# Stick-breaking attention on (key, query) blocks, with the reverse running sum as products accumulated in PSUM

## The chip, the cores and the metric

One core of one Trainium2 chip runs the whole program. The metric is the time of one execution on the device, in microseconds (us). TensorE (PE) multiplies matrices and accumulates in PSUM banks; VectorE (DVE) and ScalarE (ACT) work element by element on PSUM and SBUF; GpSimd (POOL) does the same for SBUF; SyncE (SP) issues the DMA transfers. In the traces a line such as L1129 is a line of the kernel.

## The reference

An encoder of two layers for 512 prompt frames and 64 sample frames with 1024 cached positions. Each layer is a half step of SwiGLU, a mixer of four head groups side by side on one projection, and another half step of SwiGLU:

```
x = x + 0.5 * swiglu(rmsnorm(x))
h = rmsnorm(x) @ w_in
x = x + concat[mla(h), dsa(h), stick(h), diff(h)] @ w_out
x = x + 0.5 * swiglu(rmsnorm(x))
```

The change concerns the third group, four heads of 64 dimensions:

```
z = einsum('bqhd,bkhd->bhqk', q, k) * 64 ** -0.5
mask = k_pos < q_pos
log_keep = where(mask, log_sigmoid(-z), 0)
log_after = cumsum(log_keep, axis=3, reverse=True) - log_keep
a = where(mask, exp(log_sigmoid(z) + log_after), 0)
out = einsum('bhqk,bkhd->bqhd', a, v)
```

With softplus(z) = -log_sigmoid(-z) and log_sigmoid(z) = z - softplus(z), the weight of key k is exp(z_k - sum of softplus(z_j) over the keys j >= k that the mask admits). So a running sum over the keys, from the last to the first, stands between the scores and the weights.

## The kernel before

The mixer (mix) has two stages. The first is a list of steps, PLAN: index parts, then the latent attention (mla) beside the projections of the stick group, then stick(), then the projections of the differential group (diffp) beside the top-k search of the sample, then the top-k search of the prompt (tp, lines 798 and 799 on DVE) beside the projections of the sparse group (dsap). The second stage has the product with W_out (line 915) of the first and third group beside the attention of the other two, and then W_out of these. Steps are written one after the other, and merge() interleaves the generators of one step. A scheduler then sets the order on each engine from the program's dependences and buffers, so that instructions of a later step can stand ahead of those of an earlier one. The PSUM pools hand out their banks in the order in which the program asks for them: psA has two banks (scores), psG two (projections and W_out), psT two (transposes), psQ one (transposes of queries and keys), psO one (values).

Projections go through win(): for a token tile, each of eight chunks of the input adds three products (lines 444 to 446, high and low parts of both operands) of 256 columns to one psG bank; the sample tile uses lines 432 to 435. A layer's differential and sparse projections are 1184 such products.

stick() loads keys and values, turns the keys (kT: head and dimension by key), and goes through four query tiles of 128 and two pairs of heads. For one tile and pair, scores of two heads are queries by keys (line 1129), the mask is a product that adds a triangle (line 1131), and the scaled scores are copied to SBUF by ACT (line 100). stick_weights() then works on both heads at once: minimum with 30 (line 1145, DVE), Exp and Ln on ACT (1146, 1147), maximum with z (1148, DVE), for each head a scan that sums backwards along the keys (1151, DVE), the sum with z (1152, DVE), and Exp (1153, ACT). The weights are turned to key by query through psT (line 104, copies at lines 88 and 90) and multiplied with the values (line 553). sample() does the same for a pair of heads of the 64 sample frames over 1088 keys. For a query tile, load_q() brings the queries from DRAM through tag q, which has two buffers, and qT() turns them.

The scale, the copies and the splitting of results into a high and a low part (put_o, lines 559 and 560) are helpers that all groups share.

## Time and profile before

| what | us |
|---|---|
| three runs | 2668.05, 2668.62, 2670.72 (median 2668.62) |
| profiled execution, its span | 2668.6 |
| PE busy | 2567.7 (96%) |
| DVE busy | 1471.6 (55%) |
| ACT busy | 1010.9 (38%) |
| first stick score product, layer 0 and 1 | 639.7, 1956.7 |
| first W_out product, layer 0 and 1 | 735.3, 2052.0 |
| end of the mixer, layer 0 and 1 | 911.6, 2229.1 |

A share of busy time is a mean over stages: most of the span is SwiGLU, where PE alone is full (line 324, 63% of the chain that ended last). The mixer is where other engines come near their limits, so it is read by windows of time. A matrix product with F32 operands appears as two records of the same line, one with F32R operands as one. Busy time of PE contains pipelining: the step from the start of one instruction to the start of the next tells more of its cost than its duration.

### The profile page before, as it was taken

The page shows a single profiled execution, that of the slowest core. Times are in us where ns is not written, and L with a number is a line of the kernel's source. Part 1 is how long each engine was busy: PE and PEld are TensorE (multiplying, and loading weights), DVE is VectorE, ACT ScalarE, POOL GpSimd, SP SyncE. Part 2 cuts the span into 40 slices and gives each one's busy share as a digit, 9 for nine tenths or more (in the row PEclk, how much of TensorE's full clock was granted, in tenths as well). Part 3 has the DMA queues.
Part 4 walks back from the last instruction along what each step waited for, and adds up shares of the span by engine and source line. Part 5 has one row for each costly group of instructions (what it writes and reads, how often), then busy time and mean ns, then how long its engine had stood idle before and what let it go on. Part 6 is the DMA issues. An engine that isn't in the chain of part 4 may idle for free.

```text
span 2668.6 us, 45104 instructions
## 1 busy us (share of the span) xinstructions
PE 2567.7 (96%) x18673; PEld 2407.0 (90%) x18673; DVE 1471.6 (55%) x2684; ACT 1010.9 (38%) x1915; POOL 251.6 (9%) x309
## 2 busy tenths in 40 slices
PE   8999999999898899999999999999998889999998
PEld 7999999887775899999999999988877668999998
DVE  5434344799976743433443343458899676434343
ACT  4212124645666522222332222355456664212122
POOL 0000002201410300000100000022015103000001
PEclk9999999999998999999999999999999999999999
DMA  4232323253240222222222222233342203232322
GB/s 136 80 88 80 87 74 115 61 144 90 66 120 18 85 82 85 83 84 83 84 80 86 81 86 81 88 101 91 94 116 83 82 25 95 80 87 80 88 76 72
DMA packets 424348, 227.90 MB, mean 85 GB/s; under 512 B 93980, under 2 KB 419792, under 8 KB 424144
## 3 DMA queue, kind: packets, MB, share of 16 engines
q1 hardware_dynamic: 424144, 225.02, 29.3%
q8 instruction: 147, 2.41, 0.4%
q14 instruction: 57, 0.47, 0.1%
HBM read 206.25 MB, written 18.73 MB: 84 GB/s over the span
## 4 chain that ended last, share of the span: by engine, by line
PE 83%; DVE 9%; ACT 4%; DMA 1%; issue 1%; POOL 1%; SPq 0%; ACTq 0%; DVEq 0%; POOLq 0%
PE psF L324 63%; PE psG L915 2%; PE psT L104 2%; PE psQ L104 2%; PE psO L553 2%; PE psG L444 2%; PE psG L445 2%; PE psG L446 2%; DVE P L1151 1%; PE psO L610 1%; PE psA L1000 1%; DVE P L1198 1%; ACT whl L306 1%; DVE whl L307 1%; PE psA L724 1%
## 5 line engine op out<-in xcount | busy, mean ns | idle before, releaser
L324 PE MATMUL psF<-aH,whl 128*128 128x288 f32 x5632 | 978.3, 295 | 0.0
L324 PEld LDWEIGHTS psF<-aH,whl 128*128 128x128 f32 x5632 | 825.9, 188 | 0.4 <-ACT whl L306 0.2
L306 ACT CAST whl<-raw 128x1024 fp32r<-128x1024 f32 (+2 forms) x342 | 351.7, 1028 | 1046.1 <-PE psF L324 1001.8
L324 PE MATMUL psF<-aL,whl 128*128 128x288 f32 x2816 | 602.5, 295 | 0.0
L324 PE MATMUL psF<-h,whl 128*128 128x288 f32 x4224 | 561.2, 294 | 0.0
L324 PEld LDWEIGHTS psF<-h,whl 128*128 128x128 f32 x4224 | 559.0, 188 | 0.0
L324 PEld LDWEIGHTS psF<-aL,whl 128*128 128x128 f32 x2816 | 450.2, 188 | 0.1
L307 DVE TENSOR_TENSOR whl<-raw,whl 128x1024 fp32r<-128x1024 f32 (+1 forms) x326 | 391.1, 1200 | 28.1 <-ACT whl L306 7.0
L354 DVE TENSOR_TENSOR u<-psF,R 128x576 f32<-128x576 f32 x88 | 66.7, 757 | 368.4 <-PE psF L324 368.4
L370 DVE SCALAR_TENSOR_TENSOR xT<-psF,xT 128x576 f32<-128x576 f32 x96 | 72.7, 757 | 329.1 <-PE psF L324 329.1
L444 PE MATMUL psG<-whl,aH 128*128 128x256 f32 (+1 forms) x672 | 200.4, 299 | 5.7 <-DVE gq L825 3.6
L446 PE MATMUL psG<-whl,aL 128*128 128x256 f32 (+1 forms) x672 | 202.1, 301 | 0.0
L445 PE MATMUL psG<-whl,aH 128*128 128x256 f32 (+1 forms) x672 | 198.4, 295 | 0.9 <-DVE whl L307 0.9
L269 POOL TENSOR_TENSOR ssum<-ssum,sq 128x576 f32<-128x576 f32 x24 | 36.9, 1538 | 1664.3 <-ACT sq L267 1664.3
L352 DVE TENSOR_TENSOR g<-psF,R 128x576 f32<-128x576 f32 x88 | 66.6, 757 | 206.9 <-PE psF L324 198.7
L915 PE MATMUL psG<-op,whl 128*128 128x288 f32 x768 | 133.2, 312 | 14.2 <-ACT op L1232 8.0
L444 PEld LDWEIGHTS psG<-whl,aH 128*128 128x128 f32 x672 | 127.2, 190 | 13.0 <-issue 6.3
L445 PEld LDWEIGHTS psG<-whl,aH 128*128 128x128 f32 x672 | 127.6, 190 | 6.8 <-issue 2.8
L446 PEld LDWEIGHTS psG<-whl,aL 128*128 128x128 f32 x672 | 127.5, 190 | 5.7 <-issue 4.2
L915 PEld LDWEIGHTS psG<-op,whl 128*128 128x128 f32 x768 | 110.6, 194 | 22.2 <-ACT op L1232 8.5
L357 ACT CAST h<-u 128x576 fp32r<-128x576 f32 x88 | 59.4, 674 | 167.5 <-DVE u L355 167.5
L358 DVE TENSOR_TENSOR h<-u,h 128x576 fp32r<-128x576 f32 x88 | 66.7, 758 | 63.2 <-ACT h L357 63.2
(379 smaller groups left out, 2847.6 us busy)
## 6 DMA issues: line engine op xcount, KB each, us to landing
raw<-in_w_ff_gate SPq DMA_DIRECT2D x88, 512.0 KB, 3.7
raw<-in_w_ff_up SPq DMA_DIRECT2D x88, 512.0 KB, 3.7
raw<-in_w_ff_down SPq DMA_DIRECT2D x64, 512.0 KB, 3.6
raw<-in_w_in SPq DMA_DIRECT2D x36, 512.0 KB, 3.7
raw<-in_w_ff_down SPq DMA_DIRECT2D x32, 384.0 KB, 3.2
raw<-in_w_out SPq DMA_DIRECT2D x48, 256.0 KB, 3.3
xs<-xT SPq DMA_DIRECT2D x16, 288.0 KB, 2.1
xT<-xs SPq DMA_DIRECT2D x8, 576.0 KB, 4.3
```

Source lines behind the costliest of these rows:

```text
L104: self.nc.tensor.transpose(out, in_, self.ident[:rows, :rows])
L306: self.nc.scalar.copy(hi[:, 0:n], raw[:, 0:n])
L307: (eng or self.nc.vector).tensor_tensor(lo[:, 0:n], raw[:, 0:n], hi[:, 0:n], ALU.subtract)
L324: mm = nc.tensor.matmul(ps[:, j, 0:HALF], w[c], a(c)[:, hs[j]], start=(c == 0 and p == 0), stop=(c == n - 1 and p == 2))
L352: nc.vector.tensor_tensor(j2(g), pss[0][:, :, 0:HALF], R2, ALU.mult)
L354: nc.vector.tensor_tensor(j2(u), pss[1][:, :, 0:HALF], R2, ALU.mult)
L358: nc.vector.tensor_tensor(h[:, 1, :], u, h[:, 0, :], ALU.subtract)
L370: nc.vector.scalar_tensor_tensor(j2(xv), ps[:, :, 0:HALF], 0.5, j2(xv), ALU.mult, ALU.add)
L444: nc.tensor.matmul(ps[:m, 0:n], a, hi, start=(c == 0), stop=False)
L445: nc.tensor.matmul(ps[:m, 0:n], a, lo, start=False, stop=False)
L446: nc.tensor.matmul(ps[:m, 0:n], b, hi, start=False, stop=(c == KC - 1))
L915: nc.tensor.matmul(ps[k][:, 0:HALF], wt[:, sl], a[:, hs[k]], start=(c == 0 and p == 0), stop=(c == n - 1 and p == 2))
```

## The change

stick() computes scores with keys on the partitions and queries along the row. All five query tiles are loaded and turned first, with the scale 1/8 on the way, into one buffer qT. prompt() takes a pair of heads at a time and the key blocks 3, 2, 1, 0; block b meets the queries from 128 b on, so it has 512 - 128 b columns. Scores stay in their PSUM bank: blocks 3 and 1 in psA, blocks 2 and 0 in psG. softplus() reads the bank, as Abs, Exp and Ln on ACT and one operation on DVE that adds the maximum of z and 0. Into the same bank go products of a matrix of minus ones (negones, for each later key block) and of a triangle of minus ones (negtri, for the block itself) with the softplus values; one Exp then leaves the weights key by query, as the value product takes them. sample() works alike on 9 key blocks in three banks; the later blocks' softplus values are added up by DVE before one product with negones. The scan, stick_weights(), the turning of weights and the copies of the scores go. Both new matrices and their operands are F32.

```diff
@@ -159,9 +159,11 @@
                                 base=0, channel_multiplier=1)
         self.tri = C("triR", [128, 128], F32R)
         nc.vector.tensor_copy(self.tri, tri)
-        self.triS = C("triS", [128, 64], F32R)
-        nc.vector.tensor_copy(self.triS[0:64], tri[0:64, 0:64])
-        nc.vector.tensor_copy(self.triS[64:128], tri[64:128, 64:128])
+        self.negones = C("negones", [128, 128])
+        nc.vector.memset(self.negones, -1.0)
+        self.negtri = C("negtri", [128, 128])
+        nc.gpsimd.affine_select(self.negtri, self.negones, pattern=[[-1, 128]], compare_op=ALU.is_ge, fill=0.0,
+                                base=0, channel_multiplier=1)
         self.rope64 = C("rope64", [128, 5, 2, 32])
         nc.sync.dma_start(self.rope64, I["rope64"])
         self.rope32 = C("rope32", [128, 5, 2, 16])
...
@@ -1085,75 +1087,98 @@
                 self.transpose(pt[:, pr * 128:pr * 128 + 128], kn[:, tt * 256 + pr * 128:tt * 256 + pr * 128 + 128])
             self.evac(self.turn(tt), kT3[:, :, tt * 128:tt * 128 + 128], pt[:, 0:256].rearrange("p (a n) -> p a n", a=2))
         o += self.new_o()
-        def qT(tt, m):
+        qT = self.op()[:, 0:1024].rearrange("p (a n) -> p a n", a=2)
+        for tt, (t0, m) in enumerate(TT):
             q = self.load_q("c", tt, m)
             pt = self.psQ()
             for pr in range(2):
                 self.transpose(pt[:, pr * 128:pr * 128 + m], q[:m, pr * 128:pr * 128 + 128])
-            return pt[:, 0:256]
+            p3 = pt[:, 0:256].rearrange("p (a n) -> p a n", a=2)
+            if tt < 4:
+                self.scaled(qT[:, :, t0:t0 + 128], p3, 0.125)
+            else:
+                for j in range(2):
+                    hs = slice(64 * j, 64 * j + 64)
+                    self.scaled(self.qbds[hs, :, hs], p3[hs, :, 0:64], 0.125)
+
+        def prompt(pr):
+            X, Y = [self.big() for _ in range(2)], [self.big() for _ in range(2)]
+            Z = [t([128, 512], tag="PT") for _ in range(2)]
+            off = {3: 0, 2: 128, 1: 384}
+            part = lambda T, j, b: T[j][:, off[b]:off[b] + 512 - 128 * b] if b else Z[j]
+            for b in (3, 2, 1, 0):
+                N = 512 - 128 * b
+                for j in range(2):
+                    hs = slice(64 * j, 64 * j + 64)
+                    z = (self.psA() if b % 2 else self.psG())[:, 0:N]
+                    nc.tensor.matmul(z, kT[hs, pr * 512 + 128 * b:pr * 512 + 128 * b + 128], qT[hs, pr, 128 * b:512],
+                                     start=True, stop=False)
+                    nc.tensor.matmul(z[:, 0:128], self.tri, self.identR, start=False, stop=True)
+                    sp = part(X, j, b)
+                    self.softplus(sp, z)
+                    for b2 in range(3, b, -1):
+                        nc.tensor.matmul(z[:, (b2 - b) * 128:N], self.negones, part(X, j, b2), start=False, stop=False,
+                                         skip_group_check=True)
+                    nc.tensor.matmul(z, self.negtri, sp, start=False, stop=True, skip_group_check=True)
+                    nc.scalar.activation(part(Y, j, b), z, AF.Exp)
+            po = self.psO()
+            for b in range(4):
+                for j in range(2):
+                    c0 = b * 256 + (2 * pr + j) * 64
+                    nc.tensor.matmul(po[64 * j:64 * j + 64, 128 * b:512], vn[:, c0:c0 + 64], part(Y, j, b),
+                                     start=(b == 0), stop=(b == 3))
+            self.put_o(o, pr, 0, 512, po)
 
         def sample(pr):
-            kTs, vc = sreg[pr]
             self.kT_sample("sb", pr, ksn, kTs)
             self.load_cache("sb", pr, 1, vc)
-
-            def mms(out, s):
-                new = s.start == PAST
-                nc.tensor.matmul(out, self.qbds[:, pr, :], kTs[:, s], start=True, stop=not new)
-                if new:
-                    nc.tensor.matmul(out, self.identR, self.triS, start=False, stop=True)
-            z, a = self.big(), self.big()
-            for ps, s in self.sample_scores(mms):
-                self.scaled(z[:, s], ps, 0.125)
-            self.stick_weights(z[:, 0:LS], a[:, 0:LS], [a[:, 0:LS]])
-            PT = self.pT_sample(a)
+            S, E = self.big(), self.big()
+            blk = lambda T, b: T[:, b * 128:b * 128 + 128]
+            nc.gpsimd.memset(blk(E, 7)[64:128], 0.0)
+            regs = [(self.psT()[0:64, 0:128], 8, 9), (self.psA(), 4, 8), (self.psA(), 0, 4)]
+            for z, b0, b1 in regs:
+                for b in range(b0, b1):
+                    w = 64 if b == 8 else 128
+                    nc.tensor.matmul(blk(z, b - b0), kTs[:, b * 128:b * 128 + w], self.qbds[:, pr, :],
+                                     start=(b == b0), stop=(b < 8), skip_group_check=True)
+                    if b == 8:
+                        nc.tensor.matmul(z, self.tri[0:64, 0:64], self.dupl[0][0:64, :], start=False, stop=True,
+                                         skip_group_check=True)
+                rows = slice(0, 64) if b0 == 8 else slice(0, 128)
+                sp = S[rows, b0 * 128:b1 * 128]
+                self.softplus(sp, z)
+                if b0 == 8:
+                    nc.vector.tensor_copy(blk(E, 7)[0:64], sp)
+                else:
+                    for b in range(b1 - 2, b0 - 2, -1):
+                        if b >= 0:
+                            nc.vector.tensor_tensor(blk(E, b), blk(E, b + 1), blk(S, b + 1), ALU.add)
+                    nc.tensor.matmul(z, self.negones, E[:, b0 * 128:b1 * 128], start=False, stop=False,
+                                     skip_group_check=True)
+                nc.tensor.matmul(z, self.negtri[rows, rows], sp, start=False, stop=True, skip_group_check=True)
+                nc.scalar.activation(sp, z, AF.Exp)
             po = self.psO()
-            self.av_sample(po[:, 0:128], PT, lambda j: vc[:, j * 128:j * 128 + 128], vsn[:, pr * 128:pr * 128 + 128])
+            self.av_sample(po[:, 0:128], S.rearrange("p (b n) -> p b n", n=128),
+                           lambda j: vc[:, j * 128:j * 128 + 128], vsn[:, pr * 128:pr * 128 + 128])
             for j in range(2):
                 self.put_o(o, pr, 512, 64, po[64 * j:64 * j + 64, 64 * j:64 * j + 64], 64 * j, 64 * j + 64)
 
-        sreg = [(kTs, vc)] * 2
-        p3 = qT(4, 64).rearrange("p (a n) -> p a n", a=2)
-        for j in range(2):
-            nc.scalar.copy(self.qbds[64 * j:64 * j + 64, :, 64 * j:64 * j + 64], p3[64 * j:64 * j + 64, :, 0:64])
-        for tt, (t0, m) in enumerate(TT[:4]):
+        for pr in range(2):
             yield
-            L = t0 + 128
-            q = t([128, 512], tag="qT")[:, 0:256]
-            nc.scalar.copy(q, qT(tt, m))
-            for pr in range(2):
-                z, a = self.pair(), self.pair()
-                zv, av = z[:, :, 0:L], a[:, :, 0:L]
-                for j in range(2):
-                    pa, hs = self.psA(), slice(64 * j, 64 * j + 64)
-                    nc.tensor.matmul(pa[:, 0:L], q[hs, pr * 128:pr * 128 + 128], kT[hs, pr * 512:pr * 512 + L],
-                                     start=True, stop=False)
-                    nc.tensor.matmul(pa[:, L - 128:L], self.identR, self.tri, start=False, stop=True)
-                    self.scaled(z[:, j, 0:L], pa[:, 0:L], 0.125)
-                self.stick_weights(zv, av, [a[:, j, 0:L] for j in range(2)])
-                PT = [self.pT_prompt(a[:, j, :], tt, j) for j in range(2)]
-                po = self.av_prompt(PT, lambda kt, j: vn[:, kt * 256 + (2 * pr + j) * 64:
-                                                         kt * 256 + (2 * pr + j) * 64 + 64], tt)
-                self.put_o(o, pr, t0, 128, po[:, 0:128])
-                yield
-            if tt in STICK_AT:
-                sample(STICK_AT.index(tt))
-
-    def stick_weights(self, z, a, rows):
-        """a = exp(z + reverse inclusive sum of -softplus(z)); softplus(z) = max(z, ln(1 + exp(min(z, 30))))"""
-        nc = self.nc
-        nc.vector.tensor_scalar(a, z, 30.0, None, ALU.min)
-        nc.scalar.activation(a, a, AF.Exp)
-        nc.scalar.activation(a, a, AF.Ln, bias=1.0)
-        nc.vector.tensor_tensor(a, z, a, ALU.max)
-        for r in rows:
-            rev = r[:, ::-1]
-            nc.vector.tensor_tensor_scan(rev, self.zero.to_broadcast(list(r.shape)), rev, 0.0, ALU.add, ALU.subtract)
-        nc.vector.tensor_tensor(a, z, a, ALU.add)
-        nc.scalar.activation(a, a, AF.Exp)
+            prompt(pr)
+            yield
+            sample(pr)
+
+    def softplus(self, out, z):
+
+        nc = self.nc
+        nc.scalar.activation(out, z, AF.Abs)
+        nc.scalar.activation(out, out, AF.Exp, scale=-1.0)
+        nc.scalar.activation(out, out, AF.Ln, bias=1.0)
+        nc.vector.scalar_tensor_tensor(out, z, 0.0, out, ALU.max, ALU.add)
...
-STICK_AT = (0, 1)
...
-    nc = bacc.Bacc("TRN2", target_bir_lowering=False, num_devices=1)
+    nc = bacc.Bacc("TRN2", target_bir_lowering=False, num_devices=1, dynamic_dma_scratch_size=4096)
```

Elsewhere the diff takes out comment lines alone. From line 163 on, lines are two higher in the kernel after: 444 to 446 become 446 to 448. The order of the instructions changes on all engines from the last part of the latent attention to the end of the mixer, and nowhere else.

On PE, before, in the stick group of layer 0: products of the differential projections (psG from whl) stand between a tile's transposes (psT from P), the scores of the next tile (L1129) and the values (L553).

```order
L446 MATMUL psG_7325<-whl_7314,aL_3809 128x256
L444 MATMUL psG_7325<-whl_7314,aH_3808 128x256
L104 MATMUL psT_6618<-ident,P_6601 128x128 x2
L104 MATMUL psT_6623<-ident,P_6601 128x128 x2
L445 MATMUL psG_7325<-whl_7315,aH_3808 128x256
L446 MATMUL psG_7325<-whl_7314,aL_3809 128x256
L444 MATMUL psG_7325<-whl_7320,aH_3808 128x256
L445 MATMUL psG_7325<-whl_7321,aH_3808 128x256
L1129 MATMUL psA_6748<-xT_6416,qT_6739 128x384
L553 MATMUL psO_6628<-PT_6621,xT_6416 64x128
```

Six projection products lie between the transposes and around them; in the whole group there are 254 of them.

On PE, after, in the stick group of layer 0: the scores are L1114, the mask L1116, products with the full matrix L1120 and with the triangle L1122.

```order
L1120 MATMUL psA_6704<-P_6660,negones 128x128
L1120 MATMUL psA_6704<-P_6660,negones 128x256
L1122 MATMUL psA_6704<-P_6660,negtri 128x384
L1116 MATMUL psA_6715<-identR,triR 128x128
L1114 MATMUL psG_6738<-op_6449,xT_6417 128x512
L1120 MATMUL psG_6726<-P_6660,negones 128x128
L1120 MATMUL psG_6726<-P_6660,negones 128x256
L1120 MATMUL psG_6726<-P_6660,negones 128x384
L1122 MATMUL psG_6726<-PT_6664,negtri 128x512
L1120 MATMUL psA_6715<-P_6661,negones 128x128
L1120 MATMUL psA_6715<-P_6661,negones 128x256
L1122 MATMUL psA_6715<-P_6661,negtri 128x384
```

The group's own products follow one another, those of one head pair in banks of psA and psG by turns; no projection is among them.

On PE, after, at the end of that group: the last products of the second pair's block 0, and what follows.

```order
L1120 MATMUL psG_6738<-P_6661,negones 128x128
L1120 MATMUL psG_6738<-P_6661,negones 128x256
L1120 MATMUL psG_6738<-P_6661,negones 128x384
L1122 MATMUL psG_6738<-PT_6665,negtri 128x512
L446 MATMUL psG_6861<-whl_6850,aH_3809 128x256
L447 MATMUL psG_6861<-whl_6851,aH_3809 128x256
L448 MATMUL psG_6861<-whl_6850,aL_3810 128x256
L446 MATMUL psG_6861<-whl_6850,aH_3809 128x256
L447 MATMUL psG_6861<-whl_6851,aH_3809 128x256
L448 MATMUL psG_6861<-whl_6850,aL_3810 128x256
```

The first product of the differential projections (L446, bank psG_6861) stands behind the last triangle product of the bank psG_6738; from here on 448 projection products precede the first of W_out.

## Rows read from the trace of the kernel before

**Rows 1.** The page: span, and busy us of each engine.

```profile
span 2668.6 us, 45104 instructions
PE 2567.7 (96%) x18673; PEld 2407.0 (90%) x18673; DVE 1471.6 (55%) x2684; ACT 1010.9 (38%) x1915; POOL 251.6 (9%) x309
```

**Rows 2.** Lines 1129, 915, both layers: ns min/median/max, first and last start (us).

```profile
L1129 PE MATMUL psA<-xT,qT x32: 272/481/694, 639.7 to 712.8; 64*128 64x128 f32 x8, 64*128 64x256 f32 x8, 64*128 64x384 f32 x8, 64*128 64x512 f32 x8
L915 PE MATMUL psG<-op,whl x192: 289/295/405, 735.3 to 791.9; 128*128 128x288 f32 x192
L1129 PE MATMUL psA<-xT,qT x32: 272/481/693, 1956.7 to 2029.7; 64*128 64x128 f32 x8, 64*128 64x256 f32 x8, 64*128 64x384 f32 x8, 64*128 64x512 f32 x8
L915 PE MATMUL psG<-op,whl x166: 288/296/408, 2052.0 to 2099.9; 128*128 128x288 f32 x166
```

**Rows 3.** Windows: stretch, us, busy PE, PEld, DVE, ACT, POOL, PEclk, DMA share, GB/s.

```profile
580.00:640.00 60.00, 59.98 (x419) 45.98 (x417) 52.70 (x155) 29.64 (x88) 7.11 (x13) 1.00 0.29 75
640.00:736.00 96.00, 88.95 (x626) 73.16 (x625) 93.26 (x165) 58.73 (x123) 38.76 (x44) 0.98 0.31 85
1956.00:2052.00 96.00, 89.26 (x632) 73.46 (x631) 93.76 (x168) 58.73 (x125) 39.74 (x44) 0.98 0.32 86
```

**Rows 4.** Costliest DVE lines of 640:736: busy us, mean ns | idle before.

```profile
L1151 DVE TENSOR_TENSOR_SCAN P<-zero,P 128x128 f32<-128x128 f32 (+4 forms) x18 | 18.3, 1052 | 0.0
L799 DVE MATCH_REPLACE8 S<-m,S 128x512 f32<-128x512 f32 (+1 forms) x23 | 14.6, 634 | 0.0
L798 DVE MAX8 m<-S 128x8 f32<-128x512 f32 (+1 forms) x22 | 14.3, 648 | 0.2
L1152 DVE TENSOR_TENSOR P<-P,P 128x256 f32<-128x256 f32 (+4 forms) x10 | 9.7, 970 | 0.0
L1148 DVE TENSOR_TENSOR P<-P,P 128x256 f32<-128x256 f32 (+4 forms) x10 | 9.5, 953 | 0.0
...
L1145 DVE TENSOR_SCALAR P<-P 128x256 f32<-128x256 f32 (+4 forms) x10 | 7.2, 725 | 0.0
```

**Rows 5.** The chain that ended last, in 597:640, its shares by line.

```profile
by line: PE psA L1000 14.9%; PE psO L553 12.3%; PE psT L104 11.2%; PE psA L1024 9.8%; PE psA L1023 8.4%; PE psG L446 8.3%; PE psG L444 7.9%; PE psG L445 7.1%; PE psO L610 4.2%; PE psQ L104 4.1%; PE psQ L1014 2.7%; PE psG L435 2.2%; PE psG L
```

**Rows 6.** PE's instructions in order, 615.0 to 618.3: start us, us, line.

```profile
615.01 0.28 PE L446 MATMUL psG<-whl,aL 128*128 128x256 f32 x1
615.13 0.28 PE L444 MATMUL psG<-whl,aH 128*128 128x256 f32 x1
615.25 0.28 PE L445 MATMUL psG<-whl,aH 128*128 128x256 f32 x1
615.37 1.02 PE L1023 MATMUL psA<-op,ql 128*128 128x512 f32 x2
616.23 1.04 PE L104 MATMUL psT<-ident,P 128*128 128x128 f32 x8
617.19 1.12 PE L1024 MATMUL psA<-op,qT 32*128 32x512 f32 x2
618.24 1.10 PE L553 MATMUL psO<-PT,xT 128*64 128x128 f32 x16
```

**Rows 7.** Score evictions and PSUM copies of 640:760, by form: busy us, mean ns.

```profile
L100 ACT ACTIVATE P<-psA 128x512 f32<-128x512 f32 x8 | 4.6, 592 | 0.0
...
L100 ACT ACTIVATE P<-psA 128x384 f32<-128x384 f32 x4 | 1.8, 492 | 0.0
...
L90 DVE COPY PT<-psT 128x512 f32<-128x512 f32 x2 | 1.4, 684 | 0.6 <-PE psT L104 0.6
...
L90 DVE COPY PT<-psT 128x384 f32<-128x384 f32 x2 | 1.1, 556 | 0.0
```

**Rows 8.** DMA of 600:660: the query tiles' loads, KB each, us to landing.

```profile
q<-qc SPq DMA_DIRECT2D x3, 128.0 KB, 2.1
```

**Rows 9.** Windows behind the group, columns as in rows 3.

```profile
800.00:860.00 60.00, 48.23 (x274) 33.37 (x274) 39.94 (x119) 36.77 (x105) 0.00 (x0) 0.86 0.09 23
736.00:912.00 176.00, 151.64 (x1002) 121.75 (x1003) 128.14 (x335) 113.97 (x311) 34.63 (x24) 0.94 0.25 72
```

## The prediction

> **What bounds the kernel now.** I read the shares of the engines first, then the stretch in which the changed code runs, then the chain into it, then single instructions. TensorE is busy 96% of the span of 2668.6 us [rows 1], so time is mostly PE work, and a change is worth what it does to PE's stream. The page shows one execution; its span equals the median of the three runs (2668.62) to 0.1 us and nothing lies around it, so sums made against the span hold for the median.
>
> The stick-breaking group stands between its first score product and the first W_out product: 639.7 to 735.3 us in layer 0 and 1956.7 to 2052.0 in layer 1, 95.6 and 95.3 us [rows 2]. The reader should see two full engines there: DVE busy 93.26 of 96 us and PE 88.95, ACT only 58.73 [rows 3]. Of DVE's time 44.7 us are the four operations of the running sum (L1151 18.3, L1152 9.7, L1148 9.5, L1145 7.2) and 28.9 us the top-k search (L798, L799) [rows 4]. PE can be full although its attention products wait for DVE, because projections of the differential and sparse groups (L444 to L446) are laid between them: of 1184 such products per layer, the order has 848 ahead of the first stick product, 254 inside the stick group and 82 behind it. Ahead of it, in 580:640, PE is without a gap (59.98 of 60) and DVE has 52.70 [rows 3]; projections take a quarter of the chain there (8.3+7.9+7.1+2.2%) [rows 5].
>
> **The change, part by part, for one layer.**
>
> 1. *The order of the projections.* prompt() takes both psG banks for its key blocks 2 and 0, and the pool hands banks out in program order. So in the changed order no projection stands inside the stick group; 736 are ahead of it and 448 behind it in one run, all before the first W_out product. They step by 0.12 us (615.01 to 615.13) [rows 6]. Between the first stick product and W_out PE therefore gets 448 in place of 336: 112 x 0.12 = +13.4 us. The same 13.4 us leave the stretch ahead, where they will not all be won: what remains there waits for DVE, whose work there is unchanged. Bounds: nothing, and the projections' share of the chain, 25.5% of 43 us, 11 us [rows 5]; DVE's idle time in 580:640 is 7.3 us [rows 3]. I take -6, next to the last.
>
> 2. *Products.* Gone are 40 prompt and 18 sample transposes: four (eight records) step from 616.23 to 617.19, 0.24 us each [rows 6], -13.9. New are products with minus ones: prompt 24 with the full matrix and 16 with the triangle, 5120 columns each; sample 2048 and 2304 columns; 14592 columns in all. Matrices and operands are F32 like L1023, of which 512 columns show two records and step 0.86 us (615.37 to 616.23) [rows 6]: 1.68 ns a column, +24.5. Sample scores by key block are 18 products of 128 columns at 0.24 us, 4.3 us, in place of 2176 columns, 3.7: +0.6. The prompt's own score and value products keep their columns (one of 512 columns costs 694 ns at most as a record [rows 2]; head pairs still write separate halves). Sum +11.2.
>
> 3. *DVE.* 44.7 us go. 22 softplus operations come, reading PSUM at no more than 0.684 us (a PSUM copy of 512 columns [rows 7]), under 15 us, and 14 additions of 128 columns, some 4 us. So DVE loses at least 26 us. That is worth what PE lost by waiting in the old group, 96-88.95 = 7.05 and 96-89.26 = 6.74 [rows 3]: -6.9, all of which I grant, because the new waits are counted apart.
>
> 4. *New waits.* The scores stay in their bank until softplus is back: Abs, Exp, Ln on ACT, one DVE operation, then the minus-ones products, a last Exp, and the value products. PE works in order and has no projections left to lay between. Half of the cover is the other head and the next key block. Per prompt half: the last 512-column block has three ACT passes of 0.592 us and 0.684 on DVE [rows 7], 2.5 us, with nothing ready behind it but the sample's scores; the last Exp before the value product 0.6; the 384-column block has 3x0.49+0.56 = 2.0 [rows 7], less the two products ahead of it (384 and 512 columns at 1.68 ns), 1.5: 0.5. That is 3.6, twice 7.2. The five query tiles are now loaded together through two buffers, 2.1 us to landing [rows 8], ahead of all scores; before, each stood beside the previous tile's work: +1.8. The following projections, dense as they are, wait 1.5 for weights and the first bank. Sum 10.5. Bounds: half the hand-offs hidden, 4; and 22, worked out under the second rival. The nearest row is the old window itself, with DVE still searching top-k between softplus operations, so I stay near the counted value.
>
> 5. *Elsewhere.* Over 736:912 PE is idle 176-151.64 = 24.4 us [rows 9], some of it behind DVE. A DVE that arrives with less behind it may give some back: bounds 0 and 5, taken 1. ACT loses the scaled evictions and gains three passes a block, at most 0.592 us each [rows 7]; with 58.73 us busy in 96 before [rows 3] it stays off the bound in sum, so I count nothing beyond item 4. Set-up of the two constants is a few operations, nothing.
>
> Sum per layer: 13.4+11.2-6.9+10.5-6-1 = +21.2; both layers +42.4; 2668.6+42.4 = 2711.
>
> The Trainium skill ("Perfetto Trace Analysis", Identifying the Most-Contended Engine) says to find the engine with the highest occupancy in a regime and to optimise that one first. In the old window that is DVE with 93.26 of 96 us [rows 3], which speaks for this change: by that rule 26 us less on DVE would shorten the stretch. The trace bears it only to the 7 us that PE waits there. The same page (Optimization Strategy) says that regimes with different limits may gain from being interleaved; the old order interleaves projections with DVE's scans and the new one parts them, and by that rule the change loses.
>
> **The rivals.**
>
> *Faster: the relief of DVE decides.* Place: the stretch ahead, and the two of 736:912. If the attention there falls to PE's own rate, the whole 13.4 us comes back in item 1, new waits shrink to 3, and half of the 24.4 us idle behind [rows 9] goes: 13.4+11.2-6.9+3-13.4-12 = -4.7, twice, 2659. It decides from the point where the stretches outside the group give back over 21 us a layer. For it: DVE 93.26 of 96, 52.70 of 60 [rows 3]. Against it: PE is at 59.98 of 60 ahead of the group, and in 800:860 DVE has only 39.94 of 60 [rows 9].
>
> *Slower still: PE starves in the stick group.* Its own work there is about 49 us: the 88.95 less 336 projections of 0.12 leave 48.6; item 2 makes it 59.8; some 11 of these (the last value products, part of the sample's minus ones, mask products of the sparse group) stand in the changed order behind the first of the 448 projections. Where the old kernel runs attention with hand-offs and few projections, 800:860, PE is busy 48.23 of 60 us and the granted clock is 0.86 of full speed (a mean of its levels 1.2 and 2.4 GHz), PE having waited a fifth of the time [rows 9]. At 0.80 x 0.86 the 49 us take 71, 22 us of waits in place of 9: +34.2 with the 1.5, items 1 and 5 kept, 2668.6+2x34.2 = 2737. For it: the same bank-to-bank pattern. Against it: here two heads and two pools alternate, and 512-column products of 0.86 us are long beside the gaps.
>
> The Trainium skill ("TensorE: Matmul & The Clock Gate", A second HAM failure mode: psum-queue depth-cycling) says that short idles between groups of products, as a kernel cycles through banks, make the clock swing between its two levels. The row of 800:860 agrees with its 0.86; by that rule this rival holds, and by the old window's 0.98 it does not.
>
> *No change.* The added products cost half, as single-pass ones (12.2 in place of 24.5), and the stretch ahead gives back 10 in place of 6: 21.2-12.3-4 = +4.9, with new waits of 6 instead of 10.5 +0.4: 2669. Against it: every F32 product in the trace shows two records.
>
> That the change does not do what it says is not a rival: the scans are gone from the order and the matrices are F32 in the code.
>
> **How the numbers follow.** What this kernel's measurement can tell from no change is 0.2%, 5.3 us. Chances: forecast 0.66, starving 0.21, relief of DVE 0.08, no change 0.05; so faster 0.08, same 0.05, slower 0.87. Range: low end with waits of 4, 11 back ahead and 5 behind, 13.4+11.2-6.9+4-11-5 = +5.7, 2680, which I lift to 2684 since these three would have to fall together; high end with waits of 22 and nothing back ahead or behind, 13.4+11.2-6.9+22 = 39.7, 2748.
>
> **What would show it.** Right: no projections between the stick products, 448 of them in some 53 us behind; the stretch from the first stick product to W_out 124 us instead of 95.6; DVE about 55% busy there; the first stick product about 6 us earlier; minus-ones products of two records, 0.86 us for 512 columns. Wrong: the stick part without projections under 50 us (then the waits are covered), a granted clock under 0.9 in it (the starving rival), the first stick product over 10 us earlier or the stretch behind W_out more than 5 us shorter (relief), or one record per product.

## The result and the profile after

The changed kernel takes 2752.67 us (median of 4 runs, 2743.60 to 2754.99), the kernel before in the same comparison 2669.67. The ratio is 1.0305, with a 95% interval of 1.0291 to 1.0318. That is 83 us slower, where 42 were forecast, and 4.7 us beyond the upper end of the range. The profiled execution has a span of 2749.5 us, 80.9 over that of before.

The page, first lines: PE's busy time is up by 62 us against [rows 1], DVE's down by 52.

```profile
span 2749.5 us, 45258 instructions
PE 2629.6 (96%) x18709; PEld 2432.0 (88%) x18709; DVE 1419.9 (52%) x2632; ACT 1013.7 (37%) x1950; POOL 235.9 (9%) x314
```

The stick group's scores and the W_out products, layer 0 and layer 1, as in [rows 2]:

```profile
L1114 PE MATMUL psA<-op,xT x16: 272/482/587, 638.5 to 697.1; 64*128 64x128 f32 x8, 64*128 64x384 f32 x8
L917 PE MATMUL psG<-op,whl x160: 290/296/401, 773.7 to 819.2; 128*128 128x288 f32 x160
L1114 PE MATMUL psA<-op,xT x16: 272/482/587, 1999.3 to 2051.2; 64*128 64x128 f32 x8, 64*128 64x384 f32 x8
L917 PE MATMUL psG<-op,whl x94: 288/295/402, 2127.9 to 2149.9; 128*128 128x288 f32 x94
```

From the first score to W_out there are now 135.2 and 128.6 us in place of 95.6 and 95.3. Counted from the mixer's first projection, the first score comes 1.9 us earlier in layer 0 and 0.1 in layer 1. From the first W_out product to the end of the mixer there are 4.4 and 4.5 us more. These three make 42.1 and 37.7, all but 1 us of the difference.

Windows of layer 0, columns as in [rows 3]: ahead of the group, the group, the projections behind it, and 174 of the 181 us from W_out to the end of the mixer.

```profile
580.00:638.50 58.50, 49.97 (x314) 32.16 (x312) 53.39 (x157) 28.64 (x84) 0.00 (x0) 1.00 0.27 72
638.50:708.80 70.30, 64.95 (x266) 40.62 (x267) 43.03 (x103) 34.55 (x91) 0.40 (x2) 0.83 0.07 16
708.80:773.70 64.90, 64.43 (x499) 59.64 (x497) 22.04 (x38) 25.03 (x52) 35.19 (x53) 1.00 0.51 147
773.70:948.00 174.30, 147.31 (x961) 117.19 (x960) 123.25 (x324) 111.35 (x307) 34.03 (x25) 0.94 0.19 54
```

Three things are to be seen. Ahead of the group PE was busy 59.98 of 60 us [rows 3] and is now idle 8.5 of 58.5; so the projections left and their time stayed. In the group the granted clock is 0.83, where it was 0.98. Behind it 64.9 us run dense at full clock, as forecast (448 steps of 0.12 us and the 11 us of other products, 65).

What goes before the fall of the clock shows in PE's order at the start of the group: start us, duration, instruction, and in brackets the idle time before it and who ended it.

```profile
636.40 0.41 PE L104 MATMUL psQ<-ident,q 128*128 128x128 f32 x2 [1.17 <-DMA q<-qc]
637.61 0.44 PE L104 MATMUL psQ<-ident,q 128*128 128x128 f32 x2 [0.80 <-ACT op L100]
638.52 0.79 PE L1114 MATMUL psA<-op,xT 64*128 64x128 f32 x2 [0.47 <-ACT op L100]
...
640.65 1.93 PE L104 MATMUL psT<-ident,P 128*128 128x128 f32 x8
...
644.09 3.20 PE L612 MATMUL psO<-P,op 128*128 128x128 f32 x14
```

The same stretch in windows of 2 us:

```profile
634.00:636.00 2.00, 0.76 (x4) 0.28 (x4) 1.95 (x7) 1.12 (x3) 0.00 (x0) 1.00 0.28 80
636.00:638.00 2.00, 0.80 (x4) 0.40 (x4) 1.86 (x7) 1.56 (x7) 0.00 (x0) 1.00 0.26 66
638.00:640.00 2.00, 1.53 (x5) 1.14 (x5) 1.97 (x7) 0.57 (x2) 0.00 (x0) 0.51 0.10 33
...
646.00:648.00 2.00, 2.00 (x10) 1.77 (x9) 1.81 (x6) 0.00 (x0) 0.00 (x0) 0.50 0.00 0
648.00:650.00 2.00, 2.00 (x16) 1.33 (x15) 0.27 (x2) 1.40 (x7) 0.00 (x0) 0.93 0.00 0
```

PE stands idle more than half of four microseconds while the query tiles come in and are turned through one psQ bank; then the clock is 0.50, its lower level of 1.2 GHz, up to 648. Eight records of transposes take 1.93 us there and took 1.04 before [rows 6]. The other hole is inside the group, where cached keys are turned:

```profile
PE psQ L104 <- ACT xT L88: 4.7, 2, 2.5
```

The columns are the total, the number of waits and the longest one. The copy that frees psQ stands in ACT's queue behind softplus passes. After the first of these holes the clock is 0.50 from 662 to 665, after the second from 679 to 689:

```profile
678.00:680.00 2.00, 0.28 (x2) 0.28 (x3) 2.00 (x7) 1.67 (x5) 0.00 (x0) 0.75 0.00 0
680.00:682.00 2.00, 2.00 (x6) 1.18 (x6) 2.00 (x7) 0.00 (x0) 0.00 (x0) 0.50 0.00 0
```

The group of layer 1 has a clock of 0.92; its longest slow stretch, at 0.50 from 1980 to 1993, lies ahead of the first score:

```profile
2000.00:2063.00 63.00, 59.12 (x265) 36.61 (x265) 43.28 (x105) 34.49 (x90) 0.40 (x2) 0.92 0.08 18
```

The mean clock of the whole run gives a rough size: 1 less the clock, times the span, is 29 us before (0.989) and 52 after (0.981), so at most some 23 of the 81 us are clock, and 2 of these lie behind PE's last product. Runs of the changed kernel differ in the same way: 2743.6 us at 0.985 and 2755.0 at 0.979.

### The profile page after: what moved, and what is told of

Same layout as the page of the kernel before. It is cut to its first block, busy times and chain, and to the rows that moved or that the text cites. A ratio compares the mean times of both kernels' runs of the same rounds, so it can differ in the third digit from the quotient of the medians.

```text
span 2749.5 us, 45258 instructions
## 1 busy us (share of the span) xinstructions
PE 2629.6 (96%) x18709; PEld 2432.0 (88%) x18709; DVE 1419.9 (52%) x2632; ACT 1013.7 (37%) x1950; POOL 235.9 (9%) x314
## 4 chain that ended last, share of the span: by engine, by line
PE 83%; DVE 7%; ACT 4%; POOL 2%; issue 2%; DMA 1%; SPq 0%; ACTq 0%; POOLq 0%; DVEq 0%
PE psF L326 61%; PE psG L917 3%; PE psT L104 2%; PE psQ L104 2%; PE psG L447 1%; PE psG L446 1%; PE psG L448 1%; PE psO L555 1%; PE psO L612 1%; POOL gq L398 1%; DVE whl L309 1%; POOL rt L394 1%; DVE Sw L814 1%; DVE mx L534 1%; POOL gq L399 1%
## 5 line engine op out<-in xcount | busy, mean ns | idle before, releaser
L446 PE MATMUL psG<-whl,aH 128*128 128x256 f32 (+1 forms) x672 | 197.3, 295 | 3.0 <-DVE xT L372 1.9
L448 PE MATMUL psG<-whl,aL 128*128 128x256 f32 (+1 forms) x672 | 196.1, 292 | 0.0
L446 PEld LDWEIGHTS psG<-whl,aH 128*128 128x128 f32 x672 | 126.3, 188 | 9.4 <-ACT whl L308 2.3
```

Source lines behind the costliest of these rows:

```text
L446: nc.tensor.matmul(ps[:m, 0:n], a, hi, start=(c == 0), stop=False)
L448: nc.tensor.matmul(ps[:m, 0:n], b, hi, start=False, stop=(c == KC - 1))
```

## The experiments

**The order alone.** The kernel before, with psG for the scores of the second pair:

```diff
-                    pa, hs = self.psA(), slice(64 * j, 64 * j + 64)
+                    pa, hs = (self.psG() if pr else self.psA()), slice(64 * j, 64 * j + 64)
```

> The kernel before with one edit: the scores of the second head pair take a bank of psG, where they took psA. Algorithm and work are those of before; the projections on PE then stand as in the changed kernel, 736 ahead of the stick group, none inside, 448 behind. Theory (order): the loss of 83 us comes mostly from the projections that no longer fill PE's waits. Then this kernel alone loses much: 13 us per layer of projections moved behind the group, and the old group's waits for DVE (44.7 us of running sum beside the top-k search) laid bare, some 15 to 25 us per layer: 2725 to 2745 us in all. Rival (work): the loss is the added products of minus ones and their hand-offs; the order costs little: under 2685.

Measured: 2781.6 us, ratio 1.0417 (1.0399 to 1.0434), 112 us slower and so beyond what either theory gave. The trace is of the fastest of its five executions, 2764.4 us, so the median lost more than the rows show. The windows of the old algorithm in the new order, ahead of the group, the group, and up to W_out:

```profile
580.00:636.00 56.00, 49.15 (x311) 31.89 (x309) 50.75 (x151) 26.31 (x78) 0.00 (x0) 1.00 0.27 70
636.00:704.00 68.00, 47.40 (x209) 31.53 (x210) 61.06 (x129) 31.61 (x75) 0.00 (x0) 0.70 0.09 21
704.00:777.80 73.80, 68.23 (x541) 63.72 (x541) 36.97 (x47) 31.14 (x56) 35.52 (x51) 0.95 0.46 129
```

Ahead of the group PE is idle 6.9 us, where the changed kernel has 8.5; in the group PE is idle 20.6 us and the clock is 0.70. Most of that idle time is three waits for the last Exp of the weights (L1153), which stands behind the scans:

```profile
PE psT L104 <- ACT P L1153: 15.8, 3, 10.0
```

So the order costs more than the whole change does, and in that order the new algorithm is 29 us faster than the old one.

**The new algorithm with the projections free.** The banks of key blocks 2 and 0, first in psA alone, then in psT:

```diff
-                    z = (self.psA() if b % 2 else self.psG())[:, 0:N]
+                    z = self.psA()[:, 0:N]
```

> The changed kernel with one edit: all key blocks of the prompt take their banks from psA, none from psG. In its order 859 projections stand ahead of the stick group, 171 inside and 154 behind. Theory (order): waits and the half clock go where projections fill them, the 13 us moved behind come back: 2700 to 2720 us (30 to 50 below the changed kernel), granted clock in the group over 0.95. Rival (work): two banks in place of four lengthen the hand-offs, the products stay: 2740 to 2760.

```diff
-                    z = (self.psA() if b % 2 else self.psG())[:, 0:N]
+                    z = (self.psA() if b % 2 else self.psT())[:, 0:N]
```

> The changed kernel with one edit: key blocks 2 and 0 take psT where they took psG, so four banks remain and the projections are free. 859 projections ahead, 77 or 52 inside, 248 or 275 behind. Theory (order): between the changed kernel and the one with psA alone if fillers inside the group matter most, 2710 to 2730; as good or better than that one if the four banks matter more. Rival (work): 2740 to 2755.

Measured: 2715.30 us with psA (ratio 1.0169, 1.0153 to 1.0184) and 2697.71 us with psT (1.0103, 1.0088 to 1.0118). One word in one line is worth 55 us. Windows of the kernel with psT, ahead, group, and up to W_out:

```profile
580.00:643.00 63.00, 62.49 (x440) 48.16 (x439) 55.59 (x159) 32.43 (x92) 10.49 (x17) 1.00 0.29 73
643.00:694.00 51.00, 50.91 (x271) 34.17 (x269) 42.32 (x103) 32.06 (x87) 3.55 (x5) 1.00 0.28 68
694.00:746.00 52.00, 51.96 (x362) 44.36 (x361) 19.11 (x34) 22.29 (x47) 20.03 (x30) 1.00 0.43 125
```

PE is never idle for long and the clock is 1.00 throughout; with psA it is 1.00 in the group, too. The first time lies where the theory put it; the second is below its range of fillers, on the side of the four banks. What remains is 28 us: 11.3 and 7.8 us between the mixer's first projection and W_out, where the prediction worked out 11.2 a layer for the products, and 5 and 3 us behind the first W_out product. That the first part is the products' is argued from this agreement. Four banks beat two although fewer projections lie inside the group (77 in place of 171).

**The price of the products.** The prompt's products with minus ones in one pass, first in the changed kernel, then with psT:

```diff
-            X, Y = [self.big() for _ in range(2)], [self.big() for _ in range(2)]
+            X, Y = [self.big(F32R) for _ in range(2)], [self.big() for _ in range(2)]
...
-                        nc.tensor.matmul(z[:, (b2 - b) * 128:N], self.negones, part(X, j, b2), start=False, stop=False,
+                        nc.tensor.matmul(z[:, (b2 - b) * 128:N], self.negonesR, part(X, j, b2), start=False, stop=False,
...
-                    nc.tensor.matmul(z, self.negtri, sp, start=False, stop=True, skip_group_check=True)
+                    nc.tensor.matmul(z, self.negtriR if b else self.negtri, sp, start=False, stop=True, skip_group_check=True)
```

> The changed kernel with the prompt's products with minus ones in F32R (softplus values of key blocks 3, 2 and 1 rounded to F32R, both matrices; block 0 against its own triangle stays F32): 8192 columns a layer at one pass instead of two, 6.9 us a layer by the step of 1.68 ns a column. If these products stand on PE's path, 2753 less 10 to 14 us: 2739 to 2743. If the group is bound by hand-offs and the clock, less than 4 us: over 2749.

> The changed kernel with psT in place of psG for key blocks 2 and 0 (as in the run with four banks and free projections, 2697.7 us) and with the prompt's products with minus ones in F32R for the later key blocks and the triangles of blocks 1 to 3. There PE was never idle at full clock, so 8192 columns at one pass less should show in full: 2 x 6.9 us, 2684 (2681 to 2688). If they are hidden, 2694 to 2699. Neither beats the kernel before (2669).

Measured: 2739.40 us (1.0257, 1.0238 to 1.0276), 13 less than the changed kernel, near the 13.8 that the step of 1.68 ns a column gives. That is in part luck: the two profiled executions differ by 8 us, of which 0.3 in layer 0 and 5.0 in layer 1 lie ahead of W_out, and the clock of the four runs is lower, 0.977 to 0.982 in place of 0.979 to 0.985. With psT, 2698.62 us (1.0103, 1.0088 to 1.0118), nothing less than the 2697.71 without it. In layer 0 the saving is there: from the mixer's first projection to W_out 296.9 us, where the kernel with psT has 303.4. In layer 1 it is not (306.2 and 303.7). There some 14 us run at 0.50, from 1976 to 1989; half of them, an estimate of what the lower level costs, is as much as the saving:

```profile
1966.00:1974.00 8.00, 8.00 (x64) 6.58 (x62) 7.69 (x19) 6.70 (x18) 7.14 (x8) 1.00 0.13 23
1974.00:1976.00 2.00, 2.00 (x9) 0.95 (x6) 1.60 (x6) 1.88 (x8) 0.00 (x0) 0.96 1.04 341
1976.00:1988.00 12.00, 12.00 (x33) 7.20 (x33) 7.02 (x18) 7.30 (x18) 0.00 (x0) 0.50 0.12 36
```

The clock of the runs with psT and one pass is 0.984 to 0.987, of those with psT alone 0.989 to 0.991. PE's records show no gap ahead of this fall.

**Single holes.** Five buffers for the query tiles (edit: q=2 becomes q=5 in BUFS), and the cached keys' copies on DVE:

```diff
-            self.evac(g == 0, dst[:, g * 512:g * 512 + 512], ps)
+            self.evac(g == 0 and act, dst[:, g * 512:g * 512 + 512], ps)
```

Here act is false for the stick group's keys.

> The changed kernel with five buffers for the query tiles in place of two, so that no load of a tile waits for another to be turned. In the changed kernel PE waits some 2.5 us for the third to fifth tile right ahead of the stick group, and the granted clock is 0.50 for the next 10 us in layer 0 and 7 in layer 1. Theory (a short hole, then half the clock): hole and slow stretch go, 2 + 3 to 5 us a layer: 2739 to 2745 us in all, and the clock of that stretch over 0.9. Rival: the hole only moves to the turning's copies on ACT: 2750 to 2756.

> The changed kernel with both copies of the stick group's cached keys on DVE, where one of two stood on ACT behind the softplus passes. In the changed kernel PE waits 2.2 to 2.6 us for that copy, twice in layer 0 and once in layer 1, and the clock is 0.50 for 3 to 9 us behind each. Theory (a queue of ACT holds a bank of PSUM, PE idles, clock halves): 5 to 10 us less in layer 0, 3 to 4 in layer 1: 2739 to 2745. Rival: DVE's queue with the top-k search holds the bank as long: 2749 to 2756.

Measured: 2742.60 us (1.0259, 1.0242 to 1.0276) and 2746.18 us (1.0291, 1.0260 to 1.0322), 10 and 6 less than the changed kernel; the 6 us lie within the spread of the runs (2742.17 to 2761.42, and 2743.60 to 2754.99), between the theory and the rival. The first time lies where the theory put it, but not for its reason. Its trace has the hole that the rival foresaw, on ACT's copy:

```profile
644.75 0.44 PE L104 MATMUL psQ<-ident,q 128*128 128x128 f32 x2 [1.47 <-ACT op L100]
```

and the clock is 0.50 from 646 to 656 as before. From the mixer's start to W_out it is no shorter (332.0 and 328.2 us; changed kernel 329.7 and 329.0); the gain lies behind W_out, 177.2 and 176.9 us in place of 180.8 and 181.7, and was not looked for there. In the second kernel the hole shrank as the theory said, from 4.7 us in two waits to 1.6:

```profile
683.51 0.66 PE L104 MATMUL psQ<-ident,kc 128*128 128x128 f32 x4 [0.79 <-DVE xT L90]
```

The clock is 1.00 from 680 to 700, where the changed kernel had 0.50 up to 688. Ahead of the group and at its start, though, 0.50 came back at other places (624 to 638, 645 to 655), and up to W_out layer 0 gained nothing (330.1 us from the mixer's start in place of 329.7), layer 1 5.7 (323.3).

**DVE's load.** The top-k search cut from 16 rounds to 4:

```diff
-            for _ in range(16):
+            for _ in range(4):
```

> The changed kernel with 4 rounds of the prompt's top-k search in place of 16: part of the selection of the sparse group is left out. 36 pairs of DVE operations a layer go, some 43 us. Theory (the stretch ahead of the stick group is bound by DVE, so the projections that left it were not won): the first stick product comes 6 us or more earlier after the mixer's start, and the stick group's softplus waits less: 2753 less 15 to 40 us. Rival (that stretch is bound by chains of PE and ACT): less than 4 us a layer, over 2745.

Measured: 2739.45 us (1.0257, 1.0242 to 1.0272), 13 less: too little for the theory, too much for the rival. The first stick product comes not earlier but later after the mixer's start, 200.5 and 204.7 us in place of 194.6 and 200.4. The stretch ahead of the group, this kernel:

```profile
580.00:640.00 60.00, 51.32 (x326) 33.81 (x325) 48.40 (x137) 28.86 (x84) 0.00 (x0) 1.00 0.28 72
```

and the changed kernel:

```profile
580.00:640.00 60.00, 51.44 (x318) 33.30 (x317) 54.86 (x161) 28.82 (x85) 0.00 (x0) 0.98 0.27 70
```

DVE has 6.5 us less to do in it and PE is idle as long (8.7 and 8.6 us). The latent group ends 3.8 and 6.3 us earlier, but most of that is clock: ahead of its end 3 us in place of 10 are at 0.50 in layer 0, and 10 in place of 20 in layer 1, an estimated 3 and 5 us. So DVE is not the bound of that stretch. Its holes are many short hand-offs; the costliest of the changed kernel between 580 and 638.5 (total, number of waits, longest):

```profile
PE psQ L104 <- ACT op L100: 1.3, 2, 0.8
PE psQ L104 <- DMA q<-qc: 1.2, 1, 1.2
PE psT L104 <- DVE P L1007: 1.1, 2, 0.9
```

The 13 us lie between the first score and W_out (118.4 and 123.5 us in place of 135.2 and 128.6), in layer 0 with none of the group at 0.50, where it was 23 us.

**Useless work in the holes.** Sixty products a layer that nobody reads:

```diff
             q = self.load_q("c", tt, m)
+            d = self.psG()
+            for k in range(12):
+                nc.tensor.matmul(d, self.identR, self.aH[:, k % 8, 0:512], start=True, stop=True)
             pt = self.psQ()
```

> The changed kernel with 60 products a layer (512 columns, F32R, 0.21 us each, 12.8 us together) that compute nothing of use: they write two psG banks ahead of the stick group and are read by nobody. In the order they lie among the last attention products of the latent group and among the turning of the query tiles, where the projections stood before the change. The 448 projections behind the stick group stay. Theory (this stretch is bound by hand-offs and by the half clock that follows PE's holes; products laid into the holes cost nothing and hold the clock): 2735 to 2752 us, no slower than the changed kernel, and no granted clock of 0.50 in the 20 us ahead of the first stick product and the 10 behind it. Rival (PE's work is the bound there too): 2 x 12.8 us slower, 2770 to 2780.

Measured: 2738.68 us (1.0254, 1.0241 to 1.0267). The added products step by 0.24 us, nine from 639.35 to 641.51, where 0.21 was counted:

```profile
639.35 2.32 PE L1095 MATMUL psG<-aH,identR 128*128 128x512 f32 x9
641.51 0.38 PE L104 MATMUL psQ<-ident,q 128*128 128x128 f32 x2
```

So with some 28 us more work for PE, the kernel is 14 us faster than the changed one. Its clock around the start of the group in layer 0:

```profile
630.00:640.00 10.00, 9.97 (x51) 6.16 (x50) 9.02 (x24) 3.74 (x14) 0.00 (x0) 1.00 0.60 133
640.00:650.00 10.00, 9.29 (x62) 7.05 (x61) 8.80 (x24) 4.78 (x18) 0.00 (x0) 1.00 0.09 29
```

The changed kernel there:

```profile
630.00:640.00 10.00, 6.95 (x41) 5.07 (x40) 8.74 (x27) 5.02 (x16) 0.00 (x0) 0.90 0.36 87
640.00:650.00 10.00, 10.00 (x48) 7.90 (x47) 5.03 (x14) 3.40 (x14) 0.00 (x0) 0.59 0.00 0
```

In layer 0 the holes are full and the clock stays at 1.00 up to W_out, which comes 9.0 us earlier after the mixer's start than in the changed kernel. In layer 1 it comes 0.8 us earlier: there the clock still fell for some 4 us at 2000, against the expectation, and from 2028 to 2038, inside the group. This is the experiment that tells most: where PE waited, filling it cost nothing, and in layer 0 the clock that it held was paid back.

**Projections spread over the group.** Three kernels with psT, a yield behind each block in prompt() and sample(), and

```diff
-PLAN = ([("a1", 1)], [("b", 1)], [("a2", 1)], [("q", 1)], [("mla", 0.2), ("sb", 1)], [("stick", 1)],
-        [("diffp", 0.33), ("ts", 1)], [("tsm", 0.2), ("tp", 0.7), ("dsap", 0.7)])
+PLAN = ([("a1", 1)], [("b", 1)], [("a2", 1)], [("q", 1)], [("mla", 0.2), ("sb", 1)], [("stick", 1), ("diffp", 0.8)], [("ts", 1)], [("tsm", 0.2), ("tp", 0.7), ("dsap", 0.7)])
```

> The changed kernel with psT in place of psG (2697.7 us) and with the stick group written block by block beside the differential projections (weights 1 and 0.8), so that the order has 859 projections ahead of the group, 194 inside and 131 behind, where it had 77 and 248. Theory: with psT PE was already busy and at full clock all through the group, so there is nothing left to fill: the same within 4 us, 2694 to 2701; a little less if the rows of the differential group, finished earlier, shorten the attention behind W_out (5 us a layer longer than in the kernel before): 2688 to 2694.

> As the spread order, with the prompt's products with minus ones in F32R as in the run that gave 2698.6 us. There 13.8 us of PE's work went and the time did not, while the run's mean granted clock fell from 0.990 to 0.986. Theory (what the shorter products saved was lost to the clock, because PE had holes again): with projections inside the group to fill them, the saving shows, 2680 to 2688, clock 0.989 or more. Rival (another engine, ACT with its softplus passes or the chain of hand-offs, has become the bound): 2694 to 2700.

> The spread order with F32R products (2691.0 us) and, in addition, five buffers for query tiles. In the run with five buffers alone the stretch behind W_out's first product took 176.8 to 177.1 us, where the changed kernel has 180.8 and 181.4 and the kernel before 176.3 and 177.1; the stretch ahead did not get shorter. Theory (the query loads of the differential and sparse groups, which wait for one of two buffers, make the 4 us): two times 4 us less, 2681 to 2685. Rival (that stretch got shorter in that run by chance of its order): 2689 to 2693. Neither is under the kernel before.

Measured: 2702.75 us (1.0124, 1.0110 to 1.0139) with F32, 2690.98 us (1.0078, 1.0064 to 1.0092) with F32R, and 2695.72 us (1.0094, 1.0077 to 1.0111) with five query buffers besides: 2 us above the expected range, between theory and rival, and above both. Spreading gains nothing where PE was full, as expected. With one-pass products 12 of the 13.8 us show against the spread order with F32, half of them against psT alone, and the best version of the new algorithm is still 0.8% behind the kernel before. The theory that holes had cost the saving is not borne out: the clock of the F32R runs is 0.982 to 0.989, and in layer 0 it falls with no gap in PE's records ahead:

```profile
645.00:653.00 8.00, 8.00 (x47) 5.44 (x46) 6.50 (x19) 5.63 (x22) 2.64 (x4) 1.00 0.46 132
654.00:663.00 9.00, 9.00 (x27) 5.47 (x26) 4.88 (x13) 5.66 (x13) 0.00 (x0) 0.50 0.00 1
```

The last run refutes the theory of the query buffers: behind W_out it has 181.6 and 183.4 us.

## Why the prediction was wrong

The direction and the place of the loss were right: the projections behind the group (64.9 us against 65), DVE relieved without gain (from the first score to W_out 65.1 of 135.2 us busy, 48%, where it had 97%), and the price of the products, as far as layer 0 with psT shows it (6.5 us saved for 6.9 worked out). Three terms of the sum were mis-sized. Behind the first two stand the holes in PE's stream and the clock; the cause of the third is open.

*Item 1, the stretch ahead: -6 taken, -1.9 and -0.1 measured to the first score.* Measured to the latent group's last product it is even 1.4 and 2.7 us longer. The step said that what remains there waits for DVE, and took what DVE's idle time allowed. The run with the shorter top-k search shows that DVE is not what it waits for: with 6.5 us less on DVE, PE's idle time did not move. PE has 8.5 us of holes there, and the run with useless products shows that a projection in that place was free: some 14 us a layer of work went in and the time fell. In layer 1 the clock besides was 0.50 from 1980 to 1993, ahead of the group. So moving 112 projections out gave next to nothing back, and the 13.4 us that they cost behind the group counted in full.

*Item 4, new waits: 10.5 taken, 21.9 and 15.6 measured.* The measured size is what is left of the 39.6 and 33.3 us between score and W_out after the 24.6 of products and projections and the -6.9. The hand-offs of softplus and minus ones that I counted, block by block, are hardly there: PE's idle time in the group is 5.4 us in layer 0, and 4.7 of it are two waits that I had not seen, both for the keys' copy in ACT's queue. The query tiles' wait, counted here at 1.8, is in the trace ahead of the first score (1.17 on the DMA, 0.80 and 0.47 on copies). Beside it stands the clock: one less the clock, times the stretch, is an estimated 12 us in layer 0 (0.83 over 70.3 us) and 5 in layer 1 (0.92 over 63). With PE's idle time up to W_out, 5.8 and 4.6 us, this leaves some 4 and 6 us that no run places. In layer 0 the clock falls three times, at the start of the group and in it, each time behind one of these three holes.

The second rival had this mechanism and was given 0.21. It was priced as a mean of a stretch with many hand-offs (0.80 busy, 0.86 clock, 22 us); the group ran at 0.92 busy and 0.83 clock in layer 0. That its 22 us of waits came out in layer 0 is in part luck: PE was busy for more of the time than assumed, and 4 us have no place. The rival kept the -6 ahead and the -1 behind, which is why it, too, stayed below the measured time. The Trainium skill ("TensorE: Matmul & The Clock Gate", A second HAM failure mode: psum-queue depth-cycling) names short idles between groups of products as what makes the clock swing. The rows at 634 to 648 agree for the holes of a microsecond; those of 1966:1976 and 645:653 above, where PE is busy throughout and 0.50 follows, do not show such an idle at all.

*Item 5, behind W_out: -1 taken, +4.4 and +4.5 measured.* The run with the old algorithm in the new order has 182.1 and 179.5 us there, where the kernel before has 176.4 and 177.2, so the new algorithm is not needed for it. The kernel with psT has 181.5 and 180.3 with its projections free, so the moved projections are not needed either. Late query loads were a theory that one run bore out and another refuted; the cause is open.

The faster rival asked for 13.4 us back ahead of the group and 12 behind it; neither came. The rule of the most-contended engine ("Perfetto Trace Analysis", Identifying the Most-Contended Engine, in the Trainium skill) is borne out only in part. The old algorithm, with DVE at 97%, loses 112 us to the order, the new one 55 (2697.71 to 2752.67). So where no projections cover the group the new algorithm is 29 us faster than the old one, and where they do it is 28 us slower; that DVE's relief makes the difference is argued, since no run takes work from DVE alone in the old kernel.

What I should have read from the profile of before: PE at 59.98 of 60 us and the clock at 1.00 ahead of the group, and 0.98 in it, were held by the projections between the attention's products (the run of the order alone has 0.70 in the group), and 800:860, a stretch with none of them, showed 0.86 [rows 9]. I took that as a price for the group alone and not for the stretch ahead, from which 112 projections left as well.

## What to carry to other kernels

Independent products that lie between dependent ones can be worth more than their own time: here they covered hand-offs and held PE's clock, and a change that takes their bank from them, or moves them into a lump, pays for all three. Look where the pools hand out banks before counting instructions; here psT in place of psG in one line was worth 55 us. And before saving PE's work in a stretch full of hand-offs, see whether PE is the bound there: an added product may cost nothing and a removed one may come back as a slower clock.

## What the runs showed of the hardware

Work that nobody needs made the kernel faster: some 28 us of products more, 14 us of time less, the mean clock 0.989 and in one of four runs 0.987, in place of 0.979 to 0.985. Work removed gave nothing: 13.8 us of products less, 1 us of time more, clock 0.984 to 0.987 in place of 0.989 to 0.991. And a clock of 0.50 can follow a stretch in which PE's records leave no gap at all (1966 to 1976 in the run with psT and one-pass products, 645 to 653 in the spread one); the ends of products are modelled in a trace, so a very short gap might not show. Which property of the products brings it on there was not tried.
